# A 64-byte table ahead of the normed rows: operands of TensorE at a multiple of 128 bytes

## Chip, cores and metric

One core of one Trainium2 chip. The metric is the device time of one launch, in microseconds. Five engines matter: TensorE (PE; its weight loads are shown apart, as PEld), VectorE (DVE), ScalarE (ACT), GpSimd (POOL) and SyncE (SP), whose queue issues most DMAs.

## The reference, cut to what matters

One decoder layer on 256 tokens of width 1024, in float32:

```
h    = rms_norm(x, norm1_g)
proj = h @ w_in                       # 1824 RWKV + 1536 MoBA + 2048 gate columns
y_a  = rwkv7_time_mix(shifted proj[:1824], ...)           # 8 heads of 64
y_b  = moba_attention(q, k, v from proj[1824:3360])       # 8 heads of 64
x    = x + (sigmoid(ga) * (y_a @ w_branch_a) + sigmoid(gb) * (y_b @ w_branch_b)) @ w_out
h2   = rms_norm(x, norm2_g)
a, b = split(h2 @ w_ffn_up)           # 2 x 2816 columns
x    = x + (gelu(causal_conv3(a)) * b) @ w_ffn_down
```

## The kernel before

Every large product is done in a split form: each float32 operand is written as a high part (rounded to the matmul's type) and a low part (the rest), and the product is high x high + high x low + low x high. Weights come from memory in pieces of 128 x 1024 elements (`raw`). ScalarE makes the high part (`whi`, L238) and VectorE the low one (`wlo`, L248); rings of four, four and three buffers hold them. The activations are split once and stay.

The names that matter here:

- `hx`: the normed rows, transposed, 128 partitions x 8 x 2 x 256: for each of 8 slices of the width, 256 tokens of the high part (`hh`) and 256 of the low part (`hl`). Written once from x (L393, L396) and, in the same memory, once more for the FFN (L1118, L1119).
- the by-tiles: four buffers of 128 x 1024 elements behind hx. They serve the RWKV chain (`L`, `sq`, `rx`) and the first half of the attention scores (`sc`), and last hold the branch rows: `ybh`, `ybl` (attention) and `yah`, `yal` (RWKV).
- `PC`: 128 x 16 elements, 64 bytes in a partition, decay products of the RWKV chain. One VectorE copy writes it and three VectorE instructions read it.
- `mh`, `ml`: the merged branches, split, for the output projection. `hb`: the gated FFN rows, split, in four parts of 256 tokens.

Products and their lines:

- `wst` (L278, L280, L283): weights stationary, activations moving, 256 columns a matmul. For 128 output channels L278 multiplies `whi` by `hh`, L280 the same `whi` by `hl`, over four slices, then L283 `wlo` by `hh`: 12 matmuls. It runs most of the combined projection (hx) and both branch projections (ybh and ybl, then yah and yal). L431 is the same for the first piece.
- `xst` (L299, L300, L303): activations stationary, weights moving, 512 columns: q, k and v (hx), and the output projection (mh, ml).
- `up` (L1160, L1163): weights stationary. L1160 moves `hh` and `hl` of a slice in one matmul of 512 columns, four in a row; L1163 then moves `hh` against `wlo`, four of 256 columns.
- `down` (L1178, L1180, L1182): hb stationary, weights moving, 512 columns. The last step is written out (L1240 to L1242); its last twelve matmuls have 256 columns.

Every matmul has its own weight load. After the first steps, a small planner in the code interleaves two threads, the RWKV chain with the attention, and the "bulk" of projections; from the output projection on the code runs in the order written. The FFN is 11 steps, each two `up` and one `down` of the step before.

Tiles of the pool `cst` are placed one behind the other, each at a multiple of 32 bytes in its partition, in the order in which the code asks for them; a tile is placed once and for all. Before, the order is `trig`, hx, the four by-tiles, PC, then KB (RWKV keys), the weight rings and the rest. hx begins at byte 29,760 = 232 x 128 + 64, the by-tiles at 46,144, 50,240, 54,336 and 58,432 (all 64 modulo 128), PC at 62,528, KB at 62,592 (0 modulo 128). whi, wlo, raw, hb, mh and ml begin at 0 modulo 128, and their parts that a matmul reads at multiples of 512 bytes behind that.

Of the kernel before, what the change touches and what calls it, by code (L numbers as in the profile page):

```python
# [9 lines left out]
F32 = mybir.dt.float32  # L10
# [26 lines left out]
def body(tc, x, positions, norm1_g, w_in, rwkv_mu, w_decay_up, decay_bias, w_aaa_up,  # L37
# [5 lines left out]
    with ctx:  # L43
        cst = ctx.enter_context(tc.tile_pool(name="cst", bufs=1))
# [18 lines left out]
        def t1(name, shape=(128, 256), dt=F32):  # L63
            return sb.tile(list(shape), dt, name=name, tag="c1", bufs=8)
# [267 lines left out]
                queue += [wd[:, 2 * j - 2:2 * j - 1, :], wd[:, 2 * j - 1:2 * j, :]]  # L332
        queue += [wd[:, 20:21, :], wd[:, 21:22, :]]

        hx = cst.tile([128, 8, 2, S], F32R, name="hx", tag="hx")
        hh, hl = hx[:, :, 0], hx[:, :, 1]

# [153 lines left out]
        def ch4(t):  # L491
            return t.rearrange("p a (c i) -> p a c i", i=64)
# [32 lines left out]
        def chain():  # L525
# [21 lines left out]
            for ct in range(4):  # L547
                act.activation(kp[:, ct], av[:, ct], AF.Identity, scale=col(KA + ct),
                               bias=omka[:, ct:ct + 1])
            PC = cst.tile([128, 4, 4], F32, name="PC")  # L550
            dve.tensor_copy(PC, ch4(e2)[:, :, :, 63])
            yield 0.1, 6.0

# [287 lines left out]
            for c in range(4):  # L841
# [26 lines left out]
                if c < 3:  # L868
# [5 lines left out]
                    Sn = t1("Sn", (128, 4, 64))  # L874
                    pcb = PC[:, :, c][:, :, None].to_broadcast([128, 4, 64])
                    if St is None:
# [196 lines left out]

        now_t = 0.0
        threads = [["chain", chain(), 0.0], ["bulk", bulk(), 0.0]]
        while threads:
            th = next((h for h in threads if h[2] <= now_t), None)
# [194 lines left out]
```

## Time and profile before

| | |
|---|---|
| runs | 413.76 us median of 3 (413.24 to 414.34) |
| the profiled execution | span 411.9 us from first to last instruction; no time of its own is given beside the span, and the median of the runs is 1.9 us longer |
| TensorE | 404.6 us busy, 3199 matmuls; weight loads 355.6 us |
| VectorE, ScalarE, GpSimd | 322.2, 230.8, 38.3 us busy |
| memory | 68.76 MB read, 1.44 MB written, 170 GB/s over the span |
| granted TensorE clock | 1.000 |

A row of a group gives line, engine, operation, output and inputs by their names, shapes, the count, and behind the bar the busy time in us and the mean of one in ns, then the idle time before. Matmuls overlap: one lasts longer than the distance to the next one's start. The rows of a stretch are those of instructions that lie in it.

### The profile page before, as it was taken

How to read it: one execution, taken by the hardware profiler on the slowest of the kernel's cores; microseconds unless marked ns; L12 is line 12 of the kernel's file. 1: busy time of each engine (PE TensorE's matmuls, PEld its weight loads, DVE VectorE, ACT ScalarE, POOL GpSimd, SP SyncE). 2: the span in 40 equal slices, each digit the busy share in tenths (PEclk: the TensorE clock that was granted, in tenths of full speed). 3: DMA queues.
4: the chain of work that ended last, by engine and by line, in shares of the span. 5: the costliest groups of instructions: out<-in, count | busy, mean ns of one | idle time of the engine just before them, and what ended most of it. 6: DMA issues, size and time to landing. Idle time of an engine off the chain costs nothing.

```text
span 411.9 us, 8111 instructions
## 1 busy us (share of the span) xinstructions
PE 404.6 (98%) x3199; PEld 355.6 (86%) x3199; DVE 322.2 (78%) x559; ACT 230.8 (56%) x384; POOL 38.3 (9%) x62
## 2 busy tenths in 40 slices
PE   6999999999999999999999999999999999999996
PEld 3999989888899998999988888888888888888885
DVE  2888999869557876678974898979779678797784
ACT  5799645465444765453653884646446455464450
POOL 8910070000210010120000000000000000000000
PEclk9999999999999999999999999999999999999999
DMA  8955565663483352466564555765665666656612
GB/s 247 314 190 154 156 179 157 163 171 105 95 226 94 104 155 68 146 202 198 175 197 147 160 199 183 225 202 176 199 193 171 199 200 198 200 168 199 198 53 102
DMA packets 61765, 70.72 MB, mean 172 GB/s; under 512 B 8349, under 2 KB 52195, under 8 KB 61728
## 3 DMA queue, kind: packets, MB, share of 16 engines
q1 hardware_dynamic: 60768, 69.41, 56.3%
q0 software_dynamic: 944, 0.80, 0.9%
q8 instruction: 25, 0.41, 0.4%
q14 instruction: 12, 0.10, 0.1%
q10 hardware_dynamic: 16, 0.00, 0.0%
HBM read 68.76 MB, written 1.44 MB: 170 GB/s over the span
## 4 chain that ended last, share of the span: by engine, by line
PE 89%; DVE 4%; ACT 3%; DMA 1%; issue 1%; SPq 0%; POOL 0%; ACTq 0%
PE acc L1160 15%; PE acc L1163 7%; PE acc L278 7%; PE acc L283 7%; PE acc L280 7%; PE at L1160 5%; PE acc L299 5%; PE f L1182 4%; PE acc L303 4%; PE f L1180 4%; PE acc L300 4%; PE f L1178 4%; PE at L1163 2%; ACT sc L970 2%; DMA x<-in_x_dram 1%
## 5 line engine op out<-in xcount | busy, mean ns | idle before, releaser
L238 ACT CAST whi<-raw 128x1024 fp32r<-128x1024 f32 x120 | 125.8, 1051 | 113.6 <-PE acc L1160 26.2
L248 DVE TENSOR_TENSOR wlo<-raw,whi 128x1024 fp32r<-128x1024 f32 x120 | 145.7, 1218 | 41.8 <-PE acc L1163 12.9
L1160 PE MATMUL acc<-hx,whi 128*128 128x512 f32 x264 | 72.4, 395 | 0.0
L278 PE MATMUL acc<-hx,whi 128*128 128x256 f32 x232 | 58.2, 287 | 0.0
L280 PE MATMUL acc<-hx,whi 128*128 128x256 f32 x232 | 56.0, 278 | 0.0
L1160 PEld LDWEIGHTS acc<-hx,whi 128*128 128x128 f32 x264 | 45.3, 188 | 6.3
L1163 PEld LDWEIGHTS acc<-hx,wlo 128*128 128x128 f32 x264 | 40.2, 188 | 6.1
L278 PEld LDWEIGHTS acc<-hx,whi 128*128 128x128 f32 x232 | 43.6, 188 | 1.6 <-issue 0.7
L280 PEld LDWEIGHTS acc<-hx,whi 128*128 128x128 f32 x232 | 43.7, 188 | 0.1
L1163 PE MATMUL acc<-hx,wlo 128*128 128x256 f32 x264 | 41.3, 278 | 0.0
L283 PE MATMUL acc<-hx,wlo 128*128 128x256 f32 x232 | 35.9, 277 | 0.0
L1182 PE MATMUL f<-wlo,hb 128*128 128x512 f32 x80 | 31.3, 391 | 0.0
L1180 PE MATMUL f<-whi,hb 128*128 128x512 f32 x80 | 31.2, 390 | 0.0
L1178 PE MATMUL f<-whi,hb 128*128 128x512 f32 x80 | 31.2, 390 | 0.0
L283 PEld LDWEIGHTS acc<-hx,wlo 128*128 128x128 f32 x232 | 30.7, 188 | 0.3 <-issue 0.3
L1160 PE MATMUL at<-hx,whi 128*128 128x512 f32 x88 | 24.0, 394 | 0.0
L1168 DVE TENSOR_REDUCE an<-acc 128x256 f32<-128x512 f32 x22 | 15.0, 689 | 6.5 <-PE acc L1163 5.6
L299 PE MATMUL acc<-whi,hx 128*128 128x512 f32 x48 | 19.3, 403 | 0.0
L300 PE MATMUL acc<-whi,hx 128*128 128x512 f32 x48 | 18.8, 391 | 0.0
L1182 PEld LDWEIGHTS f<-wlo,hb 128*128 128x128 f32 x80 | 15.0, 188 | 3.5 <-DVE wlo L248 0.4
L1178 PEld LDWEIGHTS f<-whi,hb 128*128 128x128 f32 x80 | 15.0, 188 | 2.8
L1180 PEld LDWEIGHTS f<-whi,hb 128*128 128x128 f32 x80 | 15.0, 188 | 2.8
(311 smaller groups left out, 700.4 us busy)
## 6 DMA issues: line engine op xcount, KB each, us to landing
raw<-in_w_ffn_up_dram SPq DMA_DIRECT2D x44, 512.0 KB, 4.3
raw<-in_w_in_dram SPq DMA_DIRECT2D x38, 512.0 KB, 4.5
raw<-in_w_ffn_down_dram SPq DMA_DIRECT2D x22, 512.0 KB, 3.3
raw<-in_w_out_dram SPq DMA_DIRECT2D x8, 512.0 KB, 4.3
x<-in_x_dram SPq DMA_DIRECT2D x8, 256.0 KB, 5.2
early<-in_w_in_dram SPq DMA_DIRECT2D x4, 512.0 KB, 9.8
raw<-in_w_branch_b_dram SPq DMA_DIRECT2D x4, 512.0 KB, 3.6
raw<-in_w_branch_a_dram SPq DMA_DIRECT2D x4, 512.0 KB, 4.1
```

Source lines behind the costliest of these rows:

```text
L238: act.copy(hi[:, :k * c], raw[:, :k * c])
L248: eng.tensor_tensor(lo[:, :n], raw[:, :n], hi[:, :n].bitcast(F32), op=OP.subtract)
L278: pe.matmul(om, wh[:, k, ms], xh[:, k0 + k], start=k0 + k + m == 0, stop=False, skip_group_check=True)
L280: pe.matmul(om, wh[:, k, ms], xl[:, k0 + k], start=False, stop=False, skip_group_check=True)
L283: pe.matmul(om, wl[:, k, ms], xh[:, k0 + k], start=False, stop=k0 + k == nk - 1 and m == n - 1, skip_group_check=True)
L299: pe.matmul(ps_[t], xh[:, K, ts], wh[:, k], start=K == 0, stop=False)
L300: pe.matmul(ps_[t], xl[:, K, ts], wh[:, k], start=False, stop=False)
L1160: pe.matmul(ps_[m], wh[:, k, ms], hx[:, k0 + k].rearrange("p a s -> p (a s)"), start=k0 + k == 0, stop=False, skip_group_check=True)
L1163: pe.matmul(ps_[m][:, 0:S], wl[:, k, ms], hh[:, k0 + k], start=False, stop=k0 + k == 7, skip_group_check=True)
L1178: pe.matmul(fin[f], hb[:, 0, i, ts], wh[:, 0, cs], start=st, stop=False, skip_group_check=f == 3)
L1180: pe.matmul(fin[f], hb[:, 1, i, ts], wh[:, 0, cs], start=False, stop=False, skip_group_check=f == 3)
L1182: pe.matmul(fin[f], hb[:, 0, i, ts], wl[:, 0, cs], start=False, stop=False, skip_group_check=f == 3)
```

## The change

PC is asked for ahead of hx, and not in the chain:

```diff
         queue += [wd[:, 20:21, :], wd[:, 21:22, :]]
 
+        PC = cst.tile([128, 4, 4], F32, name="PC")
         hx = cst.tile([128, 8, 2, S], F32R, name="hx", tag="hx")
         hh, hl = hx[:, :, 0], hx[:, :, 1]
...
                                bias=omka[:, ct:ct + 1])
-            PC = cst.tile([128, 4, 4], F32, name="PC")
             dve.tensor_copy(PC, ch4(e2)[:, :, :, 63])
             yield 0.1, 6.0
```

PC now lies at byte 29,760, hx at 29,824 = 233 x 128, the by-tiles at 46,208, 50,304, 54,400 and 58,496 (all 0 modulo 128). KB and everything behind it stay where they were, and so does everything ahead of PC. On every engine the same instructions stand in the same order with the same waits; lines behind L334 have a number one higher until L550.

## Prediction

> **What bounds the kernel now.** I read the page first: the busy times, then the chain of work that ended last.
>
> ```profile
> span 411.9 us, 8111 instructions
> PE 404.6 (98%) x3199; PEld 355.6 (86%) x3199; DVE 322.2 (78%) x559; ACT 230.8 (56%) x384; POOL 38.3 (9%) x62
> PE 89%; DVE 4%; ACT 3%; DMA 1%; issue 1%; SPq 0%; POOL 0%; ACTq 0%
> ```
>
> TensorE is busy for nearly the whole span and carries 89% of the chain. A busy PE can still be one that waits inside an instruction, so next come the waits of TensorE (from 17 us to the end, one row in all) and the busy times in two stretches: combined projection and one FFN step.
>
> ```profile
> PE pb L862 <- DVE Z L858: 0.2, 1, 0.2
> 17.20:41.60 24.40, 24.40 (x214) 23.78 (x213) 21.10 (x40) 21.37 (x39) 4.58 (x12) 1.00 0.61 187
> 286.90:303.40 16.50, 16.50 (x89) 14.18 (x88) 13.18 (x19) 8.60 (x12) 0.00 (x0) 1.00 0.62 191
> ```
>
> Columns after the stretch: length, then PE, PEld, DVE, ACT, POOL, granted clock (1.00, full), DMA share. TensorE has 0.2 us of named waits. Weight loads (PEld) fill 23.78 of 24.40 us where the matmuls have 256 columns, and 14.18 of 16.50 in an FFN step; DVE has 3.3 us to spare there and the DMA engines 38%. So the time is the number of matmuls times their pace, and a change of a few ns in the pace of one goes to the end almost one to one.
>
> **What the addresses do to the pace now.** The change moves operands by 64 bytes and no instruction. hx and the by-tiles (ybh, ybl, yah, yal) start at 64 modulo 128 now; whi, wlo, hb, mh and ml start at 0. So the trace holds pairs to compare. Groups of TensorE by shape, in stretches where it streams. The first two groups are the same lines of code, with hx (from 101.2 us) and then with mh (201.7 to 211.1 us, right behind the branch rows) as the stationary operand; the third is an FFN step.
>
> ```profile
> L299 PE MATMUL acc<-whi,hx 128*128 128x512 f32 x12 | 4.7, 391 | 0.0
> L300 PE MATMUL acc<-whi,hx 128*128 128x512 f32 x12 | 4.7, 390 | 0.0
> L303 PE MATMUL acc<-wlo,hx 128*128 128x512 f32 x13 | 4.1, 393 | 0.0
> ...
> L299 PE MATMUL acc<-whi,mh 128*128 128x512 f32 x14 | 5.4, 389 | 0.0
> L303 PE MATMUL acc<-wlo,mh 128*128 128x512 f32 x14 | 4.3, 389 | 0.0
> ...
> L1160 PE MATMUL acc<-hx,whi 128*128 128x512 f32 x24 | 6.5, 394 | 0.0
> L1163 PE MATMUL acc<-hx,wlo 128*128 128x256 f32 x24 | 3.7, 277 | 0.0
> L1182 PE MATMUL f<-wlo,hb 128*128 128x512 f32 x9 | 3.5, 389 | 0.0
> ```
>
> At 512 columns, both operands at 0 give 389 ns (mh; hb with whi), one at 64 gives 390 to 394. That speaks for the change: 2 to 5 ns a matmul. Now 256 columns: the combined projection from 23.5 us, the branch rows from 188.9 us, and the last matmuls of the kernel, from 406.87 us.
>
> ```profile
> L280 PE MATMUL acc<-hx,whi 128*128 128x256 f32 x44 | 10.5, 276 | 0.0
> ...
> L278 PE MATMUL acc<-yah,whi 128*128 128x256 f32 x32 | 7.9, 281 | 0.0
> ...
> L1242 PE MATMUL f<-wlo,hb 128*128 128x256 f32 x2 | 0.6, 283 | 0.0
> L1241 PE MATMUL f<-whi,hb 128*128 128x256 f32 x2 | 0.6, 282 | 0.0
> L1240 PE MATMUL acc<-whi,hb 128*128 128x256 f32 x2 | 0.6, 283 | 0.0
> L1240 PE MATMUL f<-whi,hb 128*128 128x256 f32 x2 | 0.6, 280 | 0.0
> ```
>
> Here the order is the other way round. With the moving rows at 64 there are two paces, 276 and 281; the only stream with both operands at 0, the tail, runs at 280 rising to 283. A duration is the pace plus a constant, as the starts of these instructions in the timeline show:
>
> ```profile
> 32.62 0.62 PE L283 MATMUL acc<-hx,wlo 128*128 128x256 f32 x4
> 33.08 0.28 PE L278 MATMUL acc<-hx,whi 128*128 128x256 f32 x1
> ...
> 407.24 0.28 PE L1240 MATMUL f<-whi,hb 128*128 128x256 f32 x1
> 407.36 0.28 PE L1241 MATMUL f<-whi,hb 128*128 128x256 f32 x1
> ```
>
> In the tail the starts are 0.12 us apart. At 276 ns four matmuls take 0.46 us (32.62 to 33.08), 0.114 each. So 283 less 276 is about 6 to 7 ns of pace. Who gives way is seen at the weight loads of the same stretches, tail and yah:
>
> ```profile
> L1240 PEld LDWEIGHTS acc<-whi,hb 128*128 128x128 f32 x2 | 0.4, 192 | 0.0
> L278 PEld LDWEIGHTS acc<-yah,whi 128*128 128x128 f32 x32 | 6.0, 189 | 0.0
> L280 PEld LDWEIGHTS acc<-hx,whi 128*128 128x128 f32 x232 | 43.7, 188 | 0.1
> ```
>
> A load beside the 283 ns matmuls takes 192 ns against 188. With 256 columns load and matmul are nearly equally long (23.78 and 24.40 us above), so a load that grows by some ns holds the next matmul back; with 512 columns it hides. That is my reading: reads of load and matmul get in each other's way, by their relative place within 128 bytes. At equal place the load loses, which costs nothing at 512 columns and 6 ns at 256; 64 bytes apart the matmul loses at 512 columns and at 256 often neither does.
>
> **The change, part by part.** All matmuls with hx or a by-tile come to lie like the tail (256 columns) or like mh and hb (512 columns). Counts and present means, over the whole run:
>
> ```profile
> L278 PE MATMUL acc<-hx,whi 128*128 128x256 f32 x232 | 58.2, 287 | 0.0
> L280 PE MATMUL acc<-hx,whi 128*128 128x256 f32 x232 | 56.0, 278 | 0.0
> L283 PE MATMUL acc<-hx,wlo 128*128 128x256 f32 x232 | 35.9, 277 | 0.0
> L280 PE MATMUL acc<-ybl,whi 128*128 128x256 f32 x32 | 7.8, 278 | 0.0
> L280 PE MATMUL acc<-yal,whi 128*128 128x256 f32 x32 | 7.9, 281 | 0.0
> ```
>
> - Combined projection at 256 columns: to 283 from 278 (L280) and 277 (L283). L278's 287 holds the first matmul behind each break, so I take L280's 278 for it. 232 x (5 + 5 + 6) = +3.7 us. Lower end: pace of the branch rows, 281: 232 x (3 + 3 + 4) = +2.3.
> - Branch rows: 96 matmuls from 278 (ybh) and 96 from 281 (yah), 96 x 5 + 96 x 2 = +0.7 us; at 281, +0.3.
> - First product (L431), 48 matmuls of the kind, partly behind ScalarE's and VectorE's making of hx: between 0 and 48 x 7 = 0.3; I take 0.1.
> - Output of q, k, v (L299 to L303), 144 matmuls: 391.3 on average to 389, -0.3 us.
> - FFN, 352 matmuls on L1160: 394 to 389, -1.8 us. 352 on L1163, in fours behind 512-column ones: the tail's first six average 281 (280, 282, 281 in the rows, the climb), so +4, +1.4 us. Return from 256 to 512 columns: 0 where the output projection follows yah at 389 from its first matmul, or some 14 ns where down follows up (rows below: three matmuls from 297.99 take 0.70 us, the next three 0.68). 88 blocks x 14 = +1.2 at most; I take 0, since a slowed 256-column stretch precedes, as with yah.
>
> ```profile
> 286.88 1.09 PE L1160 MATMUL acc<-hx,whi 128*128 128x512 f32 x4
> ...
> 297.99 0.39 PE L1178 MATMUL f<-whi,hb 128*128 128x512 f32 x1
> ...
> 298.69 0.39 PE L1178 MATMUL f<-whi,hb 128*128 128x512 f32 x1
> ...
> 299.37 0.39 PE L1178 MATMUL f<-whi,hb 128*128 128x512 f32 x1
> ...
> 303.44 0.39 PE L1160 MATMUL acc<-hx,whi 128*128 128x512 f32 x1
> ```
>
> - PC, the small table, is touched four times; nothing waits for it, and its place costs nothing.
> - The writers: VectorE and ScalarE write hx and by-tiles at other addresses. Beside each other, a target at 0 and one at 64:
>
> ```profile
> L1219 DVE TENSOR_TENSOR hb<-cv,hb 128x256 fp32r<-128x256 f32 x22 | 9.0, 418 | 0.0
> L835 DVE TENSOR_TENSOR yal<-yf,yah 128x256 fp32r<-128x256 f32 x4 | 1.7, 418 | 0.5 <-ACT yah L834 0.5
> ```
>
> Equal, so 0. A slower TensorE gives the other engines more room; it can also fill a wait, of which there is the 0.2 us above: -0.2. Sum: 3.7 + 0.7 + 0.1 - 0.3 - 1.8 + 1.4 - 0.2 = +3.6 us. The profiled execution's span is 411.9; the runs' median, 413.76, has 1.9 us around it, which stays. Forecast 413.8 + 3.6 = 417.4 us. The sum's own range: with the lower ends +1.7 (2.3 + 0.3 + 0 - 0.3 - 1.8 + 1.4 - 0.2), with the upper +5.2 (the return 1.2, all of L431 0.2 more, no wait filled 0.2): 415.5 to 419.0.
>
> **Rivals.** *Aligned is simply better.* The tail would be a short special case of 12 matmuls, and 256-column streams would settle at 276, as most do now. Then L278 to L283 gain 232 x (2 + 2 + 1) = 1.2 us, the branch rows 96 x 2 + 96 x 5 = 0.7, the FFN 352 x (5 + 1) = 2.1, L299 to L303 0.3: -4.3, 409.5 us. For it: all rows at 512 columns. Against it: the tail starts at a good pace and leaves it within three matmuls. What decides is one number, the mean at 256 columns in the combined projection: the 512-column matmuls save 2.1 us, there are 696 + 192 + 352 = 1240 of 256 columns, now at 278 on average, so at 278 + 1.7, about 279.7 ns, the sum is zero; below it this rival wins. *Only the 512-column ones move*, with 256-column streams in the two paces in their present shares: -2.1, 411.7 us. *Nothing moves*: 64 bytes isn't the cause, or gains and losses cancel, 413.8. The Trainium skill ("TensorE: Matmul & The Clock Gate", Step-by-step: what each phase is for) says that loading weights takes no read bandwidth from the running matmul, as each has its own port; by it alone no address matters and the time stays at 413.8. The rows of 389 against 394, and 192 against 188, don't agree with it.
>
> **Chances.** Slower as forecast 0.50; aligned better 0.20; only 512 columns 0.13; no change 0.15; the rest, a slowdown by something else, 0.02. Less than 0.3%, 1.2 us, can't be told from no change here. Faster 0.33, same 0.15, slower 0.52. The range must reach to the first rival, since without the two faster cases a third would lie outside: 409.5 to 419.0; the likeliest case's own range stands above.
>
> **What would show it.** Right: L280 and L283 at 281 to 283 over the whole run, loads beside them at about 190 to 192, L299 at 389, L1160 at 389 to 391 with L1163 at 280 or more, and phase one (17 to 202 us) longer by 4 us while an FFN step stays within 0.1 us of 16.56 (286.88 to 303.44 above). Wrong: L280 at 276 everywhere, an FFN step of about 16.33 us. If L1160 stays at 394, the address modulo 128 isn't what counts.

## The result, and the profile after

The changed kernel takes 417.61 us, median of 4 runs (417.56 to 419.01), against 413.81 us (413.24 to 414.34, 4 runs) for the kernel before in the same comparison: ratio 1.0102, 95% interval 1.0084 to 1.0119. The forecast was 417.4 us. The profiled spans stand 3.8 us apart, 411.9 and 415.7.

First the page of the changed kernel: span, the busy times, the chain of work that ended last.

```profile
span 415.7 us, 8111 instructions
PE 408.7 (98%) x3199; PEld 360.6 (87%) x3199; DVE 322.6 (78%) x559; ACT 230.9 (56%) x384; POOL 37.9 (9%) x62
PE 89%; DVE 4%; DMA 2%; ACT 2%; issue 1%; SPq 0%; ACTq 0%
```

The same 3199 matmuls keep TensorE busy 4.1 us longer (404.6 before), their loads 5.0 us longer (355.6); VectorE and ScalarE are where they were. Next the busy times of two equal pieces of work: the combined projection from its third piece to the first of the next group (162 matmuls on PE), and one FFN step (89). The first fence is the kernel before, the second the changed one; columns as in the prediction.

```profile
23.56:41.58 18.02, 18.02 (x162) 18.02 (x161) 14.72 (x29) 17.63 (x29) 0.00 (x0) 1.00 0.44 140
286.88:303.44 16.56, 16.56 (x89) 14.20 (x88) 13.18 (x19) 8.64 (x13) 0.00 (x0) 1.00 0.63 192
```

```profile
22.90:41.85 18.95, 18.95 (x162) 18.95 (x161) 14.93 (x29) 18.04 (x30) 0.00 (x0) 1.00 0.47 145
289.79:306.47 16.68, 16.68 (x89) 14.31 (x88) 13.18 (x19) 8.64 (x13) 0.00 (x0) 1.00 0.63 191
```

In the combined projection the weight loads fill the stretch in both (PEld equals the length) and the same work is 0.93 us longer; the FFN step is 0.12 us longer, not within the 0.1 of the forecast. The granted clock is 1.00 in all four. Now the groups of TensorE by shape over the whole run of the changed kernel, with one row of weight loads.

```profile
L280 PE MATMUL acc<-hx,whi 128*128 128x256 f32 x232 | 58.0, 283 | 0.0
L283 PE MATMUL acc<-hx,wlo 128*128 128x256 f32 x232 | 37.2, 283 | 0.0
L283 PEld LDWEIGHTS acc<-hx,wlo 128*128 128x128 f32 x232 | 31.9, 192 | 0.3 <-issue 0.3
L280 PE MATMUL acc<-yal,whi 128*128 128x256 f32 x32 | 8.0, 283 | 0.0
L300 PE MATMUL acc<-whi,hx 128*128 128x512 f32 x48 | 18.7, 390 | 0.0
L303 PE MATMUL acc<-wlo,hx 128*128 128x512 f32 x48 | 14.8, 390 | 0.0
L1160 PE MATMUL acc<-hx,whi 128*128 128x512 f32 x264 | 72.1, 394 | 0.0
L1163 PE MATMUL acc<-hx,wlo 128*128 128x256 f32 x264 | 42.3, 281 | 0.0
```

L280 and L283 stand at 283 (278 and 277 before), yal at 283 (281), the load beside them at 192: what the tail of the kernel before showed is now the pace of the projections' streams of 256 columns. q, k and v are down to 390 (391 and 393). L1163 is at 281 (278 over the whole run before). L1160, which was to fall to 389, still has 394. Two blocks of the FFN's up in the timeline, before and then after, show what becomes of it:

```profile
288.28 1.09 PE L1160 MATMUL acc<-hx,whi 128*128 128x512 f32 x4
289.21 0.62 PE L1163 MATMUL acc<-hx,wlo 128*128 128x256 f32 x4
289.67 1.09 PE L1160 MATMUL acc<-hx,whi 128*128 128x512 f32 x4
```

```profile
291.17 1.09 PE L1160 MATMUL acc<-hx,whi 128*128 128x512 f32 x4
292.10 0.63 PE L1163 MATMUL acc<-hx,wlo 128*128 128x256 f32 x4
292.57 1.09 PE L1160 MATMUL acc<-hx,whi 128*128 128x512 f32 x4
```

Start to start: the four of 512 columns take 0.93 us in both, the four of 256 take 0.46 before and 0.47 after. The starts in the trace have this finer. In the kernel before the blocks of eight take 1387 ns (median), 226, 236, 231, 236 and 118, 113, 113, 113. After, most take 1401 or 1406 ns: 233, 236, 228, 232 and 118, 119, 117, 117, or 235, 233, 236, 224 and 118, 120, 120, 120. In the streams of q, k and v the 512-column matmuls do reach 227 (six in 1360 ns, 1373 before); in the FFN most of that gain is lost behind 256 columns. The first block of a step, which follows down's 512 columns, shows it:

```profile
289.79 1.07 PE L1160 MATMUL acc<-hx,whi 128*128 128x512 f32 x4
290.69 0.64 PE L1163 MATMUL acc<-hx,wlo 128*128 128x256 f32 x4
```

By the starts its four of 512 columns take 907 ns, 227 each, where the kernel before has 934; the fours of the other blocks take 915 to 930, nearly all of them 928 to 930.

In what follows, "pace" is the distance from start to start. The fastest that any trace shows is 113.3 ns at 256 columns (twelve in 1360 ns) and 226.7 at 512; "excess" is the sum of what the matmuls of a group have above it, where distances with a break in them (more than 15 ns above the pace) are left out. "Relative place" is the moving operand's byte address less the stationary one's, modulo 256.

### The profile page after: what moved, and what is told of

Same layout as the page of the kernel before. It is cut to its first block, busy times and chain, and to the rows that moved or that the text cites. A ratio compares the mean times of both kernels' runs of the same rounds, so it can differ in the third digit from the quotient of the medians.

```text
span 415.7 us, 8111 instructions
## 1 busy us (share of the span) xinstructions
PE 408.7 (98%) x3199; PEld 360.6 (87%) x3199; DVE 322.6 (78%) x559; ACT 230.9 (56%) x384; POOL 37.9 (9%) x62
## 4 chain that ended last, share of the span: by engine, by line
PE 89%; DVE 4%; DMA 2%; ACT 2%; issue 1%; SPq 0%; ACTq 0%
PE acc L1160 12%; PE acc L278 9%; PE acc L283 9%; PE acc L280 9%; PE acc L1163 6%; PE acc L299 4%; PE acc L303 4%; PE acc L300 4%; PE f L1182 4%; PE f L1180 4%; PE f L1178 4%; PE at L1160 4%; PE at L1163 2%; DVE wlo L248 2%; DMA raw<-in_w_ffn_up_dram 1%; DMA x<-in_x_dram 1%
## 5 line engine op out<-in xcount | busy, mean ns | idle before, releaser
L1160 PE MATMUL acc<-hx,whi 128*128 128x512 f32 x264 | 72.1, 394 | 0.0
L278 PE MATMUL acc<-hx,whi 128*128 128x256 f32 x232 | 60.1, 292 | 0.0
L280 PE MATMUL acc<-hx,whi 128*128 128x256 f32 x232 | 58.0, 283 | 0.0
L1160 PEld LDWEIGHTS acc<-hx,whi 128*128 128x128 f32 x264 | 45.6, 188 | 6.5
L278 PEld LDWEIGHTS acc<-hx,whi 128*128 128x128 f32 x232 | 44.3, 191 | 1.6 <-issue 0.7
L1163 PEld LDWEIGHTS acc<-hx,wlo 128*128 128x128 f32 x264 | 40.5, 189 | 5.6
L280 PEld LDWEIGHTS acc<-hx,whi 128*128 128x128 f32 x232 | 44.4, 191 | 0.1
L1163 PE MATMUL acc<-hx,wlo 128*128 128x256 f32 x264 | 42.3, 281 | 0.0
L283 PE MATMUL acc<-hx,wlo 128*128 128x256 f32 x232 | 37.2, 283 | 0.0
L283 PEld LDWEIGHTS acc<-hx,wlo 128*128 128x128 f32 x232 | 31.9, 192 | 0.3 <-issue 0.3
L1182 PE MATMUL f<-wlo,hb 128*128 128x512 f32 x80 | 31.4, 393 | 0.3 <-DVE wlo L248 0.3
L1178 PE MATMUL f<-whi,hb 128*128 128x512 f32 x80 | 31.2, 390 | 0.0
L1160 PE MATMUL at<-hx,whi 128*128 128x512 f32 x88 | 24.0, 394 | 0.0
L1182 PEld LDWEIGHTS f<-wlo,hb 128*128 128x128 f32 x80 | 15.0, 188 | 3.9 <-DVE wlo L248 0.8
L1178 PEld LDWEIGHTS f<-whi,hb 128*128 128x128 f32 x80 | 15.0, 188 | 2.9
```

Of the source, the lines that this page charges most:

```text
L278: pe.matmul(om, wh[:, k, ms], xh[:, k0 + k], start=k0 + k + m == 0, stop=False, skip_group_check=True)
L280: pe.matmul(om, wh[:, k, ms], xl[:, k0 + k], start=False, stop=False, skip_group_check=True)
L283: pe.matmul(om, wl[:, k, ms], xh[:, k0 + k], start=False, stop=k0 + k == nk - 1 and m == n - 1, skip_group_check=True)
L1160: pe.matmul(ps_[m], wh[:, k, ms], hx[:, k0 + k].rearrange("p a s -> p (a s)"), start=k0 + k == 0, stop=False, skip_group_check=True)
L1163: pe.matmul(ps_[m][:, 0:S], wl[:, k, ms], hh[:, k0 + k], start=False, stop=k0 + k == 7, skip_group_check=True)
L1178: pe.matmul(fin[f], hb[:, 0, i, ts], wh[:, 0, cs], start=st, stop=False, skip_group_check=f == 3)
```

## Experiments

The expectations name theories. Theory 1 is that of the prediction, the relative place of load and matmul; theory 2 lets the moving rows' own place decide (at a multiple of 128 bytes they would be slow whatever the weights do). Whether the period is 128 or 256 bytes was open too.

### One stream for each pair of places

The body is replaced by streams of like matmuls on one tile X (moving) and one W (stationary), at offsets of 0 (A), 32 (B), 64 (C), 96 (D), 128 (E) and 256 bytes (F); the first letter is the moving operand's.

```python
OFF = {"A": 0, "B": 8, "C": 16, "D": 24, "E": 32, "F": 64}
...
xo, wo = OFF[a] + 512 * k, OFF[b] + 256 * (i % 8)
pe.matmul(p[0:m, 0:n], W[:, wo:wo + m], X[:, xo:xo + n], start=i == 0, ...)
...
stream("w" + a + b, [256] * 48, a, b)
stream("x" + a + b, [512] * 32, a, b)
stream("h" + a, [256] * 48, a, "A", 64)
```

> No layer is computed: streams of matmuls alone, each matmul with its own 128-column weight load, on two float32r tiles that start at a multiple of 128 bytes. First letter: byte offset of the moving operand (A 0, B 32, C 64, D 96, E 128, F 256), second letter: that of the stationary one. Streams w: 48 of 256 columns; x: 32 of 512; u: four of 512 and four of 256 in turn, as in the FFN; h: 256 columns with a weight load of 64 columns; q, r, s: 288, 320 and 384 columns. Theory 1 (relative place): what counts is the place of the two operands to each other within 128 bytes. Then w at AA, BB, CC, DD, EA, FA has a median of 283 ns, and w at CA, AC, DB, BD 276 to 281; x at AA, CC, EA, FA has 389, at CA and AC 391 to 395. Theory 2 (moving operand alone): the first letter decides; wCA and wCC are alike (276 to 281), wAA and wAC alike (283). Theory 3 (period over 128 bytes): wEA or wFA differs from wAA. The weight load as the limit (part of theories 1 and 2): hA and hC alike at about 276, and qA, qC at 290, rA, rC at 304, sA, sC at 332 (pace of 0.443 ns a column, which 276 and 389 give, plus the 162 ns that a duration has over its pace), so the address no longer counts from 288 columns on at equal place. If something else than the load is late, hA stays at 283 and hC below.

Measured: groups of this kernel by shape, 512 columns (x), 256 columns (w), and 256 columns behind a load of only 64 columns (h).

```profile
L46 PE MATMUL xAC<-X,W 128*128 128x512 f32 x32 | 7.6, 396 | 0.0
L46 PE MATMUL xEA<-X,W 128*128 128x512 f32 x32 | 7.6, 395 | 0.0
L46 PE MATMUL xCA<-X,W 128*128 128x512 f32 x32 | 7.5, 392 | 0.0
L46 PE MATMUL xFA<-X,W 128*128 128x512 f32 x32 | 7.5, 390 | 0.0
L46 PE MATMUL xAA<-X,W 128*128 128x512 f32 x32 | 7.5, 390 | 0.0
...
L46 PE MATMUL wFA<-X,W 128*128 128x256 f32 x48 | 5.9, 283 | 0.0
L46 PE MATMUL wCC<-X,W 128*128 128x256 f32 x48 | 5.9, 283 | 0.0
L46 PE MATMUL wEA<-X,W 128*128 128x256 f32 x48 | 5.9, 281 | 0.0
L46 PE MATMUL wCA<-X,W 128*128 128x256 f32 x48 | 5.8, 279 | 0.0
L46 PE MATMUL hA<-X,W 128*64 128x256 f32 x48 | 5.6, 276 | 0.0
L46 PE MATMUL hC<-X,W 128*64 128x256 f32 x48 | 5.8, 278 | 0.0
```

Equal place (AA, CC, and FA, 256 bytes apart) gives 389 to 390 at 512 columns and 283 at 256; 128 bytes apart (EA) gives 395 and 281. So the period is 256 bytes, not 128. The sign counts too: moving rows 64 bytes ahead (CA) have 392, 64 behind (AC) 396. And hA, at equal place with half the load, runs at 276: at equal place it is the load that sets 283. hC, the same with the moving rows 64 bytes ahead, was expected like hA and has 278, a pace of 116.7 ns: there the matmul is slowed even when the load is short. A miss: streams of 288, 320 and 384 columns took 294, 309 and 334 ns at equal place, 2 to 5 above what was expected; their two places differ by 2 at most, as expected.

### The by-tiles alone

```diff
         hx = cst.tile([128, 8, 2, S], F32R, name="hx", tag="hx")
+        PC = cst.tile([128, 4, 4], F32, name="PC")
         hh, hl = hx[:, :, 0], hx[:, :, 1]
...
-            PC = cst.tile([128, 4, 4], F32, name="PC")
```

> The table lies between hx and the by-tiles: hx stays at 64 modulo 128, the by-tiles are at 0 as in the changed kernel. Theories 1 and 2: the branch rows (L278 to L283 with ybh, ybl, yah, yal) go to 283 ns, the combined projection stays at 277 to 278, FFN steps stay at 16.56 us; time 413.8 + 0.7 = 414.5 us, so about 3.1 of the 3.8 us of the change are hx's. A rival by which the place of the table or of the score buffers costs the time: 417.6 here already.

Measured: 414.61 us against 414.24, ratio 1.0016, interval 1.0002 to 1.0031, so +0.1 to +1.3 us at 414. Its groups:

```profile
L280 PE MATMUL acc<-hx,whi 128*128 128x256 f32 x232 | 56.0, 278 | 0.0
L280 PE MATMUL acc<-yal,whi 128*128 128x256 f32 x32 | 8.0, 283 | 0.0
```

The moved tiles alone go to 283; hx keeps 278. In the trace the excess of the branch rows goes from 0.61 to 1.26 us and that of the combined projection stays (0.79 and 0.80): the term of the branch rows is shown, and the place of the table and of the score buffers doesn't cost the 3.8 us, as the rival had it.

### The weights 64 bytes further, without the change and with it

```diff
             raw, _, _ = raws.pop(0)
+            wp.tile([128, 16], F32, name="gap1", tag="gap1")
             hi, lo = tiles("whi"), tiles("wlo")
+            wp.tile([128, 16], F32, name="gap2", tag="gap2")
```

All weight buffers move from 128 to 192 modulo 256, and what lies behind them (mh, ml, hb) from 128 to 0. With hx left at 64 the relative place of the 256-column streams is 128; with hx moved as the change moves it (to 128) it is 192 again, as in the kernel before.

> The kernel before with the rings of weight parts (whi, wlo) moved by 64 bytes and all behind them by 128: hx, by-tiles and weights all at 64 modulo 128, hb, mh and ml at 0. Theory 1 (relative place): hx and weights are at the same place again, so 256-column rows go to 283 ns as in the changed kernel (+4.3 us in the projections, about +1 in the up-projection), and down and the output projection, now 64 bytes apart, from 389 to 394 (264 x 5 = +1.3, 96 x 3 = +0.3): 413.8 + 6.9 = 420.7 us (419 to 421.5). Theory 2 (moving operand alone): hx moves from 64 as before, the 256-column rows stay at 276 to 281; only the matmuls that move weights change, +2 us: 415.8.

> The changed kernel with the rings of weight parts (whi, wlo) moved by 64 bytes and all behind them by 128: hx and by-tiles at 0, weights at 64 modulo 128. Theory 1 (relative place): hx and weights are 64 bytes apart as before the change, so the combined projection and the branch rows are back at 276 to 281 ns, L1160 at 394; down and the output projection pay, 389 to 394 (+1.6 us), q, k, v about as before: 415.4 us (414.5 to 416.5). Theory 2 (moving operand alone): 256-column rows stay at 283 as hx moves from 0, and the matmuls that move weights pay besides: 417.6 + 2 = 419.6.

Measured: 419.59 us, ratio 1.0136 (1.0118 to 1.0155), without the change; 415.0 us, ratio 1.0027 (1.0012 to 1.0042), with it. Groups of the one and then of the other (down, L1178 to L1182 before, has its lines two further here):

```profile
L280 PE MATMUL acc<-hx,whi 128*128 128x256 f32 x232 | 57.6, 282 | 0.0
L300 PE MATMUL acc<-whi,hx 128*128 128x512 f32 x48 | 18.9, 394 | 0.0
```

```profile
L280 PE MATMUL acc<-hx,whi 128*128 128x256 f32 x232 | 56.0, 278 | 0.0
L1182 PE MATMUL f<-whi,hb 128*128 128x512 f32 x80 | 31.7, 396 | 0.0
```

Theory 2 falls: with the rows at 128 in the second kernel, L280 is at 278. What is slow there is down, 396 where it had 390: its weights moved by 64 bytes and hb, behind both gaps, by 128, so that equal place is lost. In the first kernel the rows haven't moved at all and L280 rises to 282. That q, k and v have 394 there and not 389 is a miss for a period of 128 bytes and fits 256: they are 128 apart.

### Everything behind the chain's tiles 128 bytes further

If the period were 128 bytes, this would change nothing.

```diff
+            cst.tile([128, 32], F32, name="gap")
             KB = cst.tile([128, 2112], F32, name="KB", tag="KB")
```

> The kernel before with 128 unused bytes ahead of KB: hx and by-tiles stay, all behind them moves by 128, so hx lies 64 bytes above the weights modulo 256 and no longer 64 below; down and the output projection keep equal places. Within 128 bytes nothing changes. Theory 1 as first stated (period 128): all rows as before, 413.8 us. Theory with period 256: L1160 at 391 to 392 and not 394 (352 x -2 = -0.8 us), q, k, v (L299 to L303) at 394 to 396 and not 391 (144 x 4 = +0.6), 256-column rows at 277 to 281 (0 to +2.5): 413.8 to 416.3 us, and in any case these two rows move in opposite directions.

Measured: 416.03 us against 413.35, ratio 1.0069 (1.0052 to 1.0086).

```profile
L280 PE MATMUL acc<-hx,whi 128*128 128x256 f32 x232 | 57.1, 279 | 0.0
L303 PE MATMUL acc<-wlo,hx 128*128 128x512 f32 x48 | 15.1, 395 | 0.0
```

The relative place of the 256-column streams is now +64 instead of 192: the excess of the combined projection rises from 0.79 to 2.78 us, and q, k and v go from 391 and 393 to 395. L1160, which was to gain, does (excess 1.96 to 1.33). The period is 256 bytes, and the kernel before had lain on the better side of it.

### In steps of 16 bytes

The same streams again, with the moving rows at 16 bytes times a letter's number (A 0, E 64, H 112, M 192) ahead of the weights. w follows matmuls of 512 columns, v the same behind four small ones.

```python
for d, c in enumerate("ABCDEFGHIJKLMNOP"):
    stream("x" + c, [512] * 24, 4 * d)
    wst("w" + c, 4, 4 * d)
    ...
    wst("v" + c, 4, 4 * d)
    stream("u" + c, ([512] * 4 + [256] * 4) * 4, 4 * d)
```

> No layer is computed: streams of matmuls alone, on two float32r tiles that start at the same place modulo 256 bytes. The letter is the offset of the moving operand against the stationary one in steps of 16 bytes: A 0, B 16, C 32, D 48, E 64, and so on to P 240. Streams x: 24 of 512 columns; w and v: 48 of 256 columns in the order of the projections (each weight part loaded twice, then the low parts), w behind 512-column ones, v behind four small matmuls; u: four of 512 and four of 256 in turn. From the run on coarse offsets (period 256 bytes, sign counts): x at A 389, at E (64) 391, at M (192) 395, at I (128) 395; w at A and v at A 283 throughout; w at M (the offset of hx against the weights in the kernel before) 276 or 281, if two paces are a matter of the start, 281 behind one of the two starts and 276 behind the other; u at A about 1402 ns for eight, at M 1388, at E 1384. A theory by which the offset counts only as equal or not equal gives x 395 and w 276 to 281 at all letters but A. If 16-byte lines were what counts, as every offset here is a multiple of 16, all letters would be alike.

Measured: one line of each stream's own view, with the least, the median and the greatest duration.

```profile
L41 PE MATMUL vA<-X,W x48: 277/283/386, 28.5 to 34.3; 128*128 128x256 f32 x48
L41 PE MATMUL vM<-X,W x48: 277/281/392, 305.0 to 310.7; 128*128 128x256 f32 x48
L41 PE MATMUL wM<-X,W x48: 276/276/281, 299.1 to 304.5; 128*128 128x256 f32 x48
L41 PE MATMUL vH<-X,W x48: 275/275/385, 189.8 to 195.3; 128*128 128x256 f32 x48
```

By the starts, 256 columns run at 120.0 at equal place; at 192, the place of the kernel before, at 113.3 behind the one start (wM) and at 117.8 behind the other (vM). So the two paces of the kernel before (276 and 281) can belong to one place; the two streams differ only in what ran ahead of them. 112 had 113.3 behind both. At 512 columns only equal place has 226.7; the others have 229 to 235. The pattern of the FFN has 1404 ns for its eight at equal place, 1387 at 192, and 1384 at best.

### Looking for a better version, and missing it

Two kernels built on that. The first has the FFN's pattern with the 512-column weights and the 256-column weights at places of their own (64 - hi and 1088 - lo, in elements).

```python
if i % 8 < 4:
    mm(p, i, 512, 128, 64 - hi + 256 * k + r, 64 + 512 * k, ...)
else:
    mm(p, i, 256, 128, 1088 - lo + 256 * k + r, 64 + 512 * k, ...)
```

> No layer is computed; the kernel is 48 streams of matmuls in the pattern of the FFN's up (four of 512 columns, whose stationary operand has one place, then four of 256 columns, whose stationary operand has another). aX: the 512-column ones at equal place (moving less stationary 0 modulo 256), the 256-column ones at 16 bytes times the letter's number; eX: the first at 64; hX: the first at 112. Eight matmuls have a floor of 4 x 226.67 + 4 x 113.33 = 1360 ns. Theory (each matmul's own relative place modulo 256 decides its pace): the 512-column ones run at 226.67 only at equal place, the 256-column ones at 113.3 only at 112 and 192, so aH and aM come to 1360 to 1370, the best of all, aA stays at 1404 as in the streams with one place, hH at 1384 and eE at 1384. Rival (the return from 256 to 512 columns costs its 15 to 25 ns whatever the places): aH at 1375 to 1385, no better than hH or eE. If a pair at other letters is best, the place of one kind acts on the pace of the other.

Measured, from the starts: no pair of places out of 48 takes less than 1384 ns for the eight (1384 to 1415, mean of the last four of five blocks), where the floor is 1360; aH has 1406 and aM 1400, aA 1404 and eE 1384. The theory falls. The rival is right that no pair escapes the cost of the mix, but not in its size: it gave aH 1375 to 1385.

The second gives each weight part of the real kernel a place by its use: 112 behind the moving rows in the combined projection and the branch rows, equal place for q, k and v.

```diff
+        PUT = {'w': (20, 20), 'x': (48, 48), 'y': (20, 20), 'm': (0, 0), 'u': (0, 0), 'd': (0, 0)}
...
+        def part(nm, bufs, at):
+            return wp.tile([128, 1088], F32R, name=nm, tag=nm, bufs=bufs)[:, at:at + 1024]
...
-                hi = wp.tile([128, 1024], F32R, name="whi", tag="whi", bufs=NHI)
+                hi = part("whi", NHI, PUT[use][0])
...
-                lo = wp.tile([128, 1024], F32R, name="wlo", tag="wlo", bufs=NLO)
+                lo = part("wlo", NLO, PUT[use][1])
```

(The room comes from two small tables that share memory with others; use, w to d, is passed along with each piece.)

> The kernel before, with hx and the by-tiles where they were (64 modulo 256), and each weight part put at a place of its own in a longer buffer: for the combined projection and the branch rows (256 columns) 112 bytes behind which the moving rows lie, for q, k and v (512 columns) at equal place modulo 256; the output projection and the FFN stay as before. Theory (relative place modulo 256): L280 and L283 settle at 276 in all of phase one, blocks of twelve at 1360 ns where the kernel before had 1360 and 1413 mixed, q, k and v at 389: -0.8 us in the combined projection, -0.6 in the branch rows, -0.4 in q, k and v, -1.8 in all: 412.0 beside 413.8, ratio 0.9957. Rival (the two paces of the kernel before come from where a stream starts and not from the place): blocks stay mixed, ratio 0.999 to 1.001. If the shift to buffers with another pitch disturbs something else, the FFN step leaves 16.56 us.

Measured: 416.16 us against 414.19, ratio 1.0056 (1.0038 to 1.0074): slower, against both expectations.

```profile
L285 PE MATMUL acc<-hx,whi 128*128 128x256 f32 x232 | 57.7, 282 | 0.0
L305 PE MATMUL acc<-whi,hx 128*128 128x512 f32 x48 | 18.7, 390 | 0.0
```

q, k and v at equal place have their 390. But at 112 apart the combined projection runs at 282, where the stream H had 275. So relative place alone doesn't foretell 112.

### Every pair of places, and the fast pair of 112

256 streams of 16 matmuls of 256 columns, weights at 16 bytes times the first letter's number modulo 256, moving rows at 16 times the second's.

```python
for s_, c in enumerate("ABCDEFGHIJKLMNOP"):
    for m_, e in enumerate("ABCDEFGHIJKLMNOP"):
        ...
        wst("g" + c + e, 16, 4 * s_, 4 * m_)
```

> No layer is computed; 256 streams of 16 matmuls of 256 columns in the order of the combined projection, each behind two small ones: stream gXY has its weights at 16 bytes times X's number modulo 256 and its moving rows at 16 times Y's (A is 0, P is 240). It is to tell why the projections of the run before, with moving rows 112 bytes behind the weights, ran at 119 and not at 113.3 as the stream at 112 had. There the weights lay at 208 and the rows at 64; in the stream the weights lay at 128 and the rows at 240. Theory (relative place alone): pace depends on Y less X modulo 256, so all sixteen streams at 112 run at 113.3, and the run before is unexplained. Rival 1 (weights that don't begin at a multiple of 32 bytes cost a row more to read): rows X = A, C, E, ... have the fast entries, rows B, D, F, ... none. Rival 2 (the places themselves count): fast entries follow no difference, gIP (128, 240) at 113.3 and gNE (208, 64) at 119. gIE (128, 64), the place of the kernel before, has 113.3 or 117.7.

Measured, again each stream's own view (I is 128, E 64, M 192, P 240, N 208):

```profile
L42 PE MATMUL gII<-X,W x16: 278/283/386, 331.1 to 333.0; 128*128 128x256 f32 x16
L42 PE MATMUL gIE<-X,W x16: 276/276/385, 321.9 to 323.7; 128*128 128x256 f32 x16
L42 PE MATMUL gIP<-X,W x16: 275/275/388, 347.3 to 349.1; 128*128 128x256 f32 x16
L42 PE MATMUL gNE<-X,W x16: 278/280/385, 506.9 to 508.7; 128*128 128x256 f32 x16
```

Mean paces from the starts, over the last nine matmuls of each stream, by relative place over the sixteen weight places (longer streams at equal place settle at 120.0):

| relative place (bytes) | paces (ns) |
|---|---|
| 0 | 116.6 to 120.0, mean 118.9 |
| 64 | 113.3 five times, 117.8 to 118.6 otherwise |
| 112 | 113.3 once (weights at 128), 114.0 to 119.9 otherwise |
| 128 | 118.3 to 120.3, mean 119.4 |
| 192 | 113.3 thirteen times, 115.0 to 115.6 three times |
| the other eleven | means 117.5 to 120.1 |

Nine distances still hold the settling of some streams. Over the last four, all sixteen streams at 192 are at 113.3 to 113.5. At 112 the eight with weights at a multiple of 32 bytes are, and the other eight stay at 116.8 or 120.0. At 64 five are, all with weights at an odd multiple of 16, and at no other relative place is any.

So relative place alone doesn't decide, as rival 2 has it: gIP is fast, gNE is not. Rival 1 fails as stated, since at 64 and 192 weights at odd multiples of 16 are fast as well; at 112 it draws the line where the streams have it. That fits the kernel before this one, whose weights lay at 208, an odd multiple. And 192, which all sixteen pairs have fast here, is the place of the kernel before the change. The second kernel of this pair takes the pair (128, 240) into the real kernel:

```diff
-            return cst.tile(list(shape), dt, name=name, tag="by", bufs=4)
+            t = cst.tile([128, 1088], dt, name=name, tag="by", bufs=4)[:, 60:1084]
+            return t.rearrange("p (a b) -> p a b", a=shape[1])
...
-        hx = cst.tile([128, 8, 2, S], F32R, name="hx", tag="hx")
+        hx = cst.tile([128, 4144], F32R, name="hx", tag="hx")[:, 44:4140]
+        hx = hx.rearrange("p (k a s) -> p k a s", k=8, a=2)
```

> The kernel before with hx and the by-tiles put at 240 modulo 256 (64 before), the weights left at 128: relative place 112 with the same two places as the fast stream. Theory (these two places decide): L280 and L283 at 276 in all of phase one, blocks of twelve at 1360, the FFN's blocks at 1384 as in the stream there (1387 before): -0.8 in the combined projection, -0.6 in the branch rows, -0.2 in the FFN, q, k, v within 0.3: 412.2 beside 413.8, ratio 0.996. Rival (112 apart isn't fast in this kernel, whatever the places, as the run before had it): L280 at 282, +2 us, 415.8, ratio 1.005.

Measured: 413.8 against 413.42, ratio 1.0006 (0.9993 to 1.0018). No gain.

```profile
L282 PE MATMUL acc<-hx,whi 128*128 128x256 f32 x232 | 56.1, 277 | 0.0
L302 PE MATMUL acc<-whi,hx 128*128 128x512 f32 x48 | 18.9, 395 | 0.0
```

112 is fast in the kernel with this pair (L282 at 277, the branch rows' excess 0.09 us where it was 0.61). The combined projection keeps an excess of 1.07 (0.79 before), and q, k and v lose 0.5 us (excess 0.86 against 0.37), so no gain is left.

### The rows aligned, the weights moved to 192 apart

The last kernel keeps the change and moves only the weights of the 256-column products and of up by 64 bytes, so that these are 192 apart again, while q, k, v, the output projection and down stay at equal place.

```diff
+        PUT = {'w': (16, 16), 'x': (0, 0), 'y': (16, 16), 'm': (0, 0), 'u': (16, 16), 'd': (0, 0)}
...
         PC = cst.tile([128, 4, 4], F32, name="PC")
         hx = cst.tile([128, 8, 2, S], F32R, name="hx", tag="hx")
```

> The changed kernel (hx and the by-tiles at 128 modulo 256) with the weights of the products that move hx or a by-tile in 256 columns (combined projection, branch rows, FFN up) put 64 bytes further, at 192; for q, k and v, the output projection and down they stay at 128, at equal place. Theory (relative place modulo 256, each product for itself; 192 is the one place at which 13 of 16 streams of 256 columns ran at 113.3): the 256-column products go back to what the kernel before had or better (+0.8 us over the floor in the combined projection, 0.0 to 0.6 in the branch rows), the FFN step to 16.56, while q, k and v keep the changed kernel's 389 to 390 (0.1 over the floor against 0.4): 413.0 to 413.8, ratio to the kernel before 0.998 to 1.000; the whole loss of the change is given back with the rows aligned. Rival (rows that begin at a multiple of 128 bytes cost time in themselves): 417.6 stays. If L1160 stays at 394 and L1163 goes back to 277, the residue of the FFN's pattern belongs to its mix of sizes.

Measured: 413.14 against 413.29, ratio 0.9994 (0.9984 to 1.0003).

```profile
L285 PE MATMUL acc<-hx,whi 128*128 128x256 f32 x232 | 56.0, 278 | 0.0
L285 PE MATMUL acc<-yal,whi 128*128 128x256 f32 x32 | 7.6, 276 | 0.0
L305 PE MATMUL acc<-whi,hx 128*128 128x512 f32 x48 | 18.7, 390 | 0.0
L1165 PE MATMUL acc<-hx,whi 128*128 128x512 f32 x264 | 72.5, 395 | 0.0
```

The whole loss of the change is gone with hx and the by-tiles where the change put them, at a multiple of 128 bytes: L285 (L280 before) has 278 again, yal 276, and q, k, v keep the changed kernel's 390. A row's own alignment costs nothing; its place against the weights does. Its median is the lowest of all the layer's kernels run here, but the interval doesn't make it faster than the one before.

## Why the prediction was right, and where not

By stage, in the profiled executions (first projection of L278, first matmul on mh, first of up, last matmul):

| stage | forecast | measured |
|---|---|---|
| start to L278 (with L431) | +0.1 | -0.86 |
| phase one to the output projection | +3.9 (3.7 + 0.7 - 0.3 - 0.2) | +2.98 |
| output projection | 0 | +0.05 |
| FFN | -0.4 (1.4 - 1.8) | +1.62 |
| sum | +3.6 | +3.79 |

The mechanism and the direction were right: the 256-column streams went to the pace of the tail, by the place of load and matmul to each other. That the sum came within 0.2 us is luck: the FFN cost 2.0 us more than forecast, phase one 0.9 less, and the start, 1.0 less, came earlier for a reason outside the change as far as the runs show. Term by term, with the excess in the two traces:

- **Combined projection**, +3.7 forecast: 0.79 to 4.22, +3.4. Right, at the value taken and not at the lower end. The unbroken blocks of twelve take 1433 to 1441 ns, where the kernel before had mostly 1360 and some 1413.
- **Branch rows**, +0.7: 0.61 to 1.26, +0.65, and the same in the trace of the by-tiles alone, where the runs' ratio gives +0.1 to +1.3.
- **L431**, +0.1: +0.2. **q, k, v**, -0.3: -0.2. **L1163**, +1.4: 0.53 to 1.77, +1.2.
- **L1160**, -1.8: 1.96 to 1.73, -0.2. This is the step that failed. Streams at equal place do run at 389 to 390, and so do the fours that follow down, but not fours between fours of 256 columns. The return was given as 0 to 1.2 us and taken as 0, since the output projection follows yah at 389 from its start. That row was one of the kernel before, with yah 192 apart. In the changed kernel yah is at equal place, and the first six of the output projection take 1387 ns where they took 1360 (396 ns for the first, not 389). So 1.6 us of the 1.8 didn't come, more than the upper end of the return. The prediction's sign that the address doesn't count (L1160 staying at 394) came too, but it had this cause. The return shows at the head of each down as well (excess 0.19 to 0.49, +0.3), for which the sum had no term; a new wait adds another 0.3 (shown below).
- **Waits filled**, -0.2: -0.87. Phase one's streams grew by 3.85 us and the stage by 2.98. The rest is in the gaps of TensorE beside the streams: at the scores (-0.22), where a projection ends (-0.21), at the matmul behind Z (-0.19, the wait the prediction named), and at some smaller ones. The one named wait of the changed kernel is new, in the FFN, +0.3:

```profile
PE f L1182 <- DVE wlo L248: 0.3, 1, 0.3
```

- **The start**, not in the sum: L278 begins at 16.33 us and not at 17.19. The eight loads of x took 5.2 us to landing in the profiled execution of the kernel before and 4.3 in that of the changed one. In seven other kernels profiled here, hx moved or not, they took 4.1 to 4.6 and L278 began at 16.0 to 17.0; so this varies from execution to execution, and hx's place isn't what sets it.
- **Within 128 bytes** was too short a rule. The period is 256 bytes and the sign counts: 64 bytes ahead and 64 behind, alike in the prediction, differ. Equal place, to which the change brought everything, is the same by both, which is why the forecast held.

The rival in which alignment is simply better needed a mean of less than 279.7 at 256 columns; L280 has 283. The rival that no address matters, by the Trainium skill's sentence on two ports ("TensorE: Matmul & The Clock Gate", Step-by-step: what each phase is for), doesn't agree with the runs: 413.8, 415.0, 416.0, 417.6 and 419.6 us for the same instructions at other addresses. These are medians of three comparisons, in which the kernel before had 413.4 to 414.2. That load and matmul hinder each other is shown by the dependence on their relative place, and hA shows which one sets the pace at equal place: with half the load it goes from 120.0 back to 113.3. How they do so inside the chip no run shows.

Open: why 192 is fast and 64 and 112 only with some weights, what in the start of a stream chooses between 113.3 and 117.8 at one place, and what exactly a matmul of 512 columns pays behind 256-column ones. The tables describe it; no run explains it.

## What to carry to other kernels

Where float32 weight loads are nearly as long as the matmuls that hide them, look at the byte address of the moving operand less that of the stationary one, modulo 256: a round, aligned layout can put all streams at equal place, which was the best here for 512 columns and one of the worst for 256. Moving a small table can cost a per cent in this way, and 64 bytes ahead of the weights give it back. Price a pattern that mixes sizes from a stretch with that mix at the new places, not from pure streams of its parts.

## What the runs showed of the hardware that was not expected

- A 256-byte period with a sign: at 512 columns 390 ns at 0 and at 256, 395 at 128, 392 at +64 and 396 at -64.
- At 256 columns the one relative place that was fast with all sixteen places of the weights is 192 (113.3 to 113.5 ns over the last four distances). 112 was fast with the eight at a multiple of 32 bytes, 64 with five of the other eight.
- One place can have two paces, 113.3 and 117.8 ns, kept through a whole stream of 48, by what ran ahead of it (two streams).
- A mixed pattern of four matmuls of 512 and four of 256 columns took on average 1384 ns or more, 24 above the floor of its parts, at each of 48 pairs of places.
- In the changed kernel, behind yah at equal place (pace 120.0), the first six matmuls of the output projection took 1387 ns, 27 over their own pace; in the kernel before, behind yah 192 apart (117.7), they took 1360.
